# Modulation vectors of a diffusion step: weights as the stationary operand, in spans of 384 columns

## The chip, the cores and the metric

One core of one Trainium2 chip runs the program. The metric is the device time of one execution in microseconds (us). The program was timed three times before the change, and one more execution was taken by the profiler.

## What is computed

The kernel does one step of a two-layer model on 384 tokens of 1024 features: 128 context tokens and 256 latent tokens. Each layer modulates its tokens with nine vectors per conditioning, where there are two conditionings: one for the context tokens, one for the latent ones.

```python
def _layer(x, cond, P, l, h0):
    mod = (jax.nn.silu(cond) @ P['w_mod'][l] + P['b_mod'][l]).reshape(cond.shape[0], N_MOD, 1, D_MODEL)
    sh1, sc1, gt1, sh2, sc2, gt2, sh3, sc3, gt3 = [mod[:, i] for i in range(N_MOD)]
    h = _rmsnorm(x, P['norm_g'][l, 0]) * (1.0 + sc1) + sh1
    x = x + 0.5 * gt1 * _swiglu(h, P['ffn_w1'][l, 0], P['ffn_w2'][l, 0])
    h = _rmsnorm(x, P['norm_g'][l, 1]) * (1.0 + sc2) + sh2
    y, h_final = _mixer(h, P, l, h0)
    x = x + gt2 * y
    h = _rmsnorm(x, P['norm_g'][l, 2]) * (1.0 + sc3) + sh3
    x = x + 0.5 * gt3 * _swiglu(h, P['ffn_w1'][l, 1], P['ffn_w2'][l, 1])
    return x, h_final
```

The matrix `w_mod` has 1024 rows and 9216 columns in each of the two layers, in float32 (75.5 MB in all). A conditioning is one row, so the product is a matrix times two vectors.

## The kernel before

**The main stream.** All tokens are kept feature major (128 features by 384 tokens per tile). The weights of the FFNs and the mixer come from HBM as units of 512 KB through three buffers `wr`, issued by the queue of SP (SyncE). ACT rounds a unit to its upper half `wh` (line 126) and DVE makes the rest `wl` (line 105); both have three buffers. PE then does three matmuls for each block of 128 by 128 weights (lines 198 to 200: upper by upper, upper weights by lower tokens, lower weights by upper tokens), 24 for a unit. The weights are the stationary operand, the 384 tokens move.

**Order.** PE runs in the order in which the code is written. ACT, DVE and SP are also in written order in the opening section; behind it a scheduler orders them. The loads of weights and modulation have high priority once `settled` has run (`ahead()`). Side work is written as generators and added with `track(generator, rate, start)`; `tick()` is called between pieces of the main stream and advances each generator by its rate, from its start tick on.

**The modulation** (`mod_group`, lines 354 to 406). A group is 2048 columns. For each of eight blocks of 128 rows it loads two tiles of 128x1024 into buffers `m6` (four of them; `modw`) and issues four matmuls into four bands of 32 rows of one bank: the stationary operand is `silu_c` (128x32, of which two columns are the conditionings), and the weights move, 512 columns per band (line 386). One such step lies in one tick. At the end ACT copies the bank (line 396), PE transposes it in blocks of 128 columns (line 138), and four DVE adds put bias and result into `mod`. The last group of a layer has 1024 columns and 256 per band. The first 2048 columns of layer 0 are needed at once and are done in two halves of 1024 columns (256 per band), loaded as eight tiles each: rows 0 to 511 in `m6`, the others in `c4` (five buffers). `First.half` then makes the hidden vectors `hh` and `hl` of that half.

**The wide pieces** (`mod_wide`, lines 409 to 438). Columns 2048 to 6143 of layer 1 are made in four pieces of 1024 columns on DVE: for each conditioning a sum `macc` over the eight row blocks, multiplied by the conditioning's number of each partition (ACT for the first block, DVE `scalar_tensor_tensor` for the other seven). Then eight matmuls with the stationary `pick` sum over partitions (line 428), and the result is copied and transposed as above.

**Others that the prediction names.** `token_sums` (line 468) sums squares over partitions: stationary is a block of 32 tokens by 128 partitions, moving is one column of ones, in four bands. Line 1172 is a matmul of the mixer with 128x32 stationary and 48 moving columns. `cacc` is a sum of the mixer's convolution, on DVE.

Of the kernel before, what the change touches and what calls it, by code (L numbers as in the profile page):

```python
# [19 lines left out]
P = 128  # L20
# [36 lines left out]
def hybrid_step(ctx: ExitStack, tc: tile.TileContext, I, pos_r, pos_c, y_prompt, y_sample, new_state):  # L57
# [31 lines left out]
    def c4(shape, name):  # L89
        return sp.tile(shape, F32, tag="c4", name=name, bufs=5)  # L90
# [7 lines left out]
    def m6(shape, name, dt=F32):  # L98
        return mx.tile(shape, dt, tag="m6", name=name, bufs=4)
# [254 lines left out]
    def mod_group(l, q):  # L354

        half = isinstance(q, tuple)
        if half:
            c0 = q[1] * 512
            starts = [c0, c0 + 256, D + c0, D + c0 + 256]
            parts = [I["w_mod"][l][:, :MG].rearrange("r (a b c) -> r a b c", a=2, b=2)[:, :, q[1], :]]  # L360
        else:
            n = min(MG, NMOD * D - q * MG)
            starts = [q * MG + i * n // 4 for i in range(4)]
            parts = [I["w_mod"][l][:, q * MG + c : q * MG + c + WU] for c in range(0, n, WU)]
        w = WU * len(parts) // 4
        nb = w // P

        def load(k):
            raws = []
            for src in parts:  # L370
                raw = c4([P, WU], "modw") if half and k > 3 else m6([P, WU], "modw")
                dst = raw.rearrange("p (a c) -> p a c", a=2) if half else raw
                with ahead():
                    nc.sync.dma_start(dst, src[k * P : (k + 1) * P])
                raws.append(raw)
            return raws

        if half:
            loaded = [load(k) for k in range(KD)]
            yield  # L380
        b = ax_bank()
        for k in range(KD):
            raws = loaded[k] if half else load(k)
            for s in range(4):
                i, c = divmod(s * w, WU)
                pe.matmul(  # L386
                    b[32 * s : 32 * s + 32, :w],
                    silu_c[:, k, :],
                    raws[i][:, c : c + w],
                    start=(k == 0),  # L390
                    stop=(k == KD - 1),
                    skip_group_check=True,
                )
            yield
        ev = sp.tile([P, 512], F32, tag="c2", name="modev", bufs=7)
        act.activation(ev[:, :w], b[:, :w], AF.Copy)
        yield
        b2 = ax_bank()
        for j in range(nb):
            transpose(b2[:, j * P : (j + 1) * P], ev[:, j * P : (j + 1) * P], P)  # L400
        src = b2[:, :w].rearrange("p (b s r) -> p b s r", s=4, r=32)
        for s, c0 in enumerate(starts):
            j0 = c0 // P
            bias = bm_t[l][:, j0 : j0 + nb].unsqueeze(2).to_broadcast([P, nb, 2])
            add(mod_t[l][:, j0 : j0 + nb, :], src[:, :, s, 0:2], bias)

    pick = cst.tile([P, 2, 32], F32, tag="pick", name="pick")
    pool.memset(pick, 0.0)
    for s_ in range(2):
        pool.memset(pick[:, s_, s_ : s_ + 1], 1.0)  # L410

    def mod_wide(l, c0, n=WU):

        acc = [c4([P, WU], f"macc{s}") for s in range(2)]
        for k in range(KD):
            raw = m6([P, WU], "modw")
            nc.sync.dma_start(raw, I["w_mod"][l][k * P : (k + 1) * P, c0 : c0 + WU])
            for s in range(2):
                if k == 0:
                    act.activation(acc[s], raw, AF.Copy, scale=silu_c[:, k, s : s + 1])  # L420
                else:
                    stt(acc[s], raw, silu_c[:, k, s : s + 1], acc[s])
                yield
        w = WU // 4
        b = ax_bank()
        for i in range(2):
            for s in range(4):
                pe.matmul(
                    b[32 * s : 32 * s + 32, :w],
                    pick[:, i, :],  # L430
                    acc[i][:, s * w : (s + 1) * w],
                    start=(i == 0),
                    stop=(i == 1),
                    skip_group_check=True,
                )
        yield
        mod_out(l, b, [c0 + s * w for s in range(4)], w)
        yield

    def mod_out(l, b, starts, w):  # L440
        nb = w // P
        ev = sp.tile([P, 512], F32, tag="c2", name="modev", bufs=7)
        act.activation(ev[:, :w], b[:, :w], AF.Copy)
        b2 = ax_bank()
        for j in range(nb):
            transpose(b2[:, j * P : (j + 1) * P], ev[:, j * P : (j + 1) * P], P)
        src = b2[:, :w].rearrange("p (b s r) -> p b s r", s=4, r=32)
        for s, c0 in enumerate(starts):
            j0 = c0 // P
            bias = bm_t[l][:, j0 : j0 + nb].unsqueeze(2).to_broadcast([P, nb, 2])  # L450
            add(mod_t[l][:, j0 : j0 + nb, :], src[:, :, s, 0:2], bias)
# [1195 lines left out]
    def mod_all(l, qs, after):  # L1647
        for q in qs:
            yield from mod_group(l, q)
            after(l, q)  # L1650

    def mod_wides(l, qs, after):
        for q in qs:
            for c0 in range(q * MG, min((q + 1) * MG, NMOD * D), WU):
                yield from mod_wide(l, c0)
            after(l, q)

    def after_mod(l, q):
        if isinstance(q, tuple):
            norm_scale(l, 0, 4 * q[1], 4 * q[1] + 4)  # L1660
        elif q == 0:
            norm_scale(l, 0)
        elif q == 1:
            gate_scale(l, 0)
        elif q == 2:
            norm_scale(l, 1)
            gate_scale(l, 1)
        elif q == 3:
            norm_scale(l, 2)
        else:  # L1670
            gate_scale(l, 2)

# [50 lines left out]
    mods = mod_all(0, [(0, 0)], after_mod)  # L1723
    with tc.manual_schedule(engines={mybir.EngineType.Activation, mybir.EngineType.DVE, mybir.EngineType.SP}):
# [21 lines left out]
        rest = mod_all(0, [(0, 1)], after_mod)  # L1746
# [28 lines left out]
    for l in range(DEPTH):  # L1775
        if l == 0:
            track(mod_all(0, [1], after_mod), 0.6)
            track(mod_all(0, [2, 3], after_mod), 0.4, 20)
            track(tables(0), 1.9, 8)
        else:  # L1780
            track(tables(1), 1.6, 8)
            track(mod_all(1, [3, 4], after_mod), 0.5, 10)
        nxt = Lead(l, 1)
        ffn(l, 0, 0, ld, nxt, None if l else more)
        ld, nxt = nxt, Lead(l, 2)
        mixer(l, ld, nxt)
        if l == 0:
            track(mod_all(0, [4], after_mod), 1.0)
            track(mod_all(1, [0], after_mod), 0.4, 14)
            track(mod_wides(1, [1, 2], after_mod), 1.2, 4)  # L1790
        ld, nxt = nxt, Lead(l + 1, 0) if l + 1 < DEPTH else Final()
        ffn(l, 1, 2, ld, nxt)
        ld = nxt
# [59 lines left out]
```

## Time and profile before

| | us |
|---|---|
| median of three runs | 1774.3 |
| lowest, highest | 1772.38, 1775.49 |
| profiled execution, its own time | 1775.03 |
| profiled execution, its span | 1773.0 |
| PE busy | 1743.7 (98%) |
| DVE busy | 1246.8 (70%) |
| ACT busy | 795.8 (45%) |
| POOL busy | 203.5 (11%) |

The span reaches from the first to the last recorded instruction; 2.0 us of the execution's own time lie around it. The shares are means over the whole span. A record whose row says "x8" stands for eight records that follow each other with nothing between them. Matmuls overlap: their durations overlap those of their neighbours, so the distance from start to start is what counts.

### The profile page before, as it was taken

What the parts mean: (1) busy time and instruction counts of PE and PEld (TensorE: products, weight loads), DVE (VectorE), ACT (ScalarE), POOL (GpSimd) and SP (SyncE); (2) the same over time, 40 slices, a digit from 0 to 9 for tenths busy, and PEclk for the clock granted to TensorE, in tenths of its full rate; (3) what the DMA queues carried; (4) which work ended last, traced back from release to release, by engine and by line L of the source; (5) the groups of instructions that cost most, each with busy time, mean ns of one, the idle gap of its engine ahead of it and who ended that gap; (6) DMA issues with size and microseconds to landing.
All of it is one profiled execution on the core that took longest, in us unless ns stands there. A gap on an engine that the chain in (4) does not pass through costs nothing.

```text
span 1773.0 us, 30946 instructions
## 1 busy us (share of the span) xinstructions
PE 1743.7 (98%) x12116; PEld 1652.8 (93%) x12116; DVE 1246.8 (70%) x2344; ACT 795.8 (45%) x1330; POOL 203.5 (11%) x400
## 2 busy tenths in 40 slices
PE   7999999999999999999999999999999999999997
PEld 4899999999999989999999899999999999999997
DVE  5496676778986885678487666767799788544435
ACT  3344333575355553233366233336744546423233
POOL 2012343310010000000001133232100000000000
PEclk9999999999999999999999999999999999999999
DMA  9778788776753677788346776667666443444332
GB/s 343 249 224 275 231 252 269 226 198 190 240 157 108 186 238 228 237 280 257 112 131 208 234 224 215 175 195 233 162 210 200 131 123 116 132 130 127 123 125 77
DMA packets 253753, 344.48 MB, mean 194 GB/s; under 512 B 22399, under 2 KB 216651, under 8 KB 253608
## 3 DMA queue, kind: packets, MB, share of 16 engines
q1 hardware_dynamic: 228504, 299.18, 53.4%
q0 software_dynamic: 17088, 39.51, 7.5%
q10 hardware_dynamic: 8016, 3.82, 0.8%
q8 instruction: 95, 1.56, 0.4%
q14 instruction: 50, 0.41, 0.1%
HBM read 309.75 MB, written 32.70 MB: 193 GB/s over the span
## 4 chain that ended last, share of the span: by engine, by line
PE 81%; DVE 10%; ACT 4%; DMA 3%; issue 2%; SPq 0%; ACTq 0%; DVEq 0%
PE mm L198 25%; PE mm L200 25%; PE mm L199 25%; PE ax L386 3%; DVE wl L105 3%; DVE cacc L123 2%; DMA wr<-in_w_gate_dram 1%; DVE m_t L105 1%; PE tb L138 1%; ACT wh L126 1%; DVE m_hh L105 1%; DMA modw<-in_w_mod_dram 1%; DVE macc L123 1%; DMA wr<-in_w_in_dram 1%; ACT zp L1125 0%
## 5 line engine op out<-in xcount | busy, mean ns | idle before, releaser
L105 DVE TENSOR_TENSOR wl<-wr,wh 128x1024 fp32r<-128x1024 f32 (+2 forms) x389 | 457.0, 1175 | 352.1 <-ACT wh L126 347.4
L126 ACT ACTIVATE wh<-wr 128x1024 fp32r<-128x1024 f32 (+1 forms) x387 | 395.9, 1023 | 613.9 <-PE mm L199 443.9
L198 PE MATMUL mm<-hh,wh 128*128 128x384 f32 x1840 | 625.3, 340 | 2.7 <-ACT hh L621 2.7
L200 PE MATMUL mm<-hh,wl 128*128 128x384 f32 x1840 | 617.1, 335 | 4.4 <-DVE wl L105 4.2
L199 PE MATMUL mm<-hl,wh 128*128 128x384 f32 x1840 | 616.3, 335 | 0.5 <-DVE hl L105 0.3
L198 PEld LDWEIGHTS mm<-hh,wh 128*128 128x128 f32 x1840 | 345.9, 188 | 31.7 <-issue 18.1
L200 PEld LDWEIGHTS mm<-hh,wl 128*128 128x128 f32 x1840 | 345.8, 188 | 6.7 <-DVE wl L105 6.7
L199 PEld LDWEIGHTS mm<-hl,wh 128*128 128x128 f32 x1840 | 345.9, 188 | 1.2 <-DVE hl L105 1.1
L198 PE MATMUL mm<-ah,wh 128*128 128x384 f32 x800 | 273.2, 342 | 0.0
L199 PE MATMUL mm<-al,wh 128*128 128x384 f32 x800 | 269.4, 337 | 0.8 <-DVE al L105 0.8
L200 PE MATMUL mm<-ah,wl 128*128 128x384 f32 x800 | 270.0, 338 | 0.0
L198 PEld LDWEIGHTS mm<-ah,wh 128*128 128x128 f32 x800 | 150.2, 188 | 10.2 <-issue 6.7
L199 PEld LDWEIGHTS mm<-al,wh 128*128 128x128 f32 x800 | 150.4, 188 | 1.7 <-DVE al L105 1.1
L200 PEld LDWEIGHTS mm<-ah,wl 128*128 128x128 f32 x800 | 150.2, 188 | 0.0
L123 DVE SCALAR_TENSOR_TENSOR x<-mm,gt,x 128x128 f32<-128x128 f32 x224 | 83.1, 411 | 33.3 <-PE mm L200 33.1
L198 PE MATMUL mm<-xh,wh 128*128 128x386 f32 x240 | 84.7, 353 | 0.0
L126 ACT ACTIVATE ah<-av 128x384 fp32r<-128x384 f32 x82 | 42.1, 519 | 89.4 <-DVE av L105 89.1
L200 PE MATMUL mm<-xh,wl 128*128 128x386 f32 x240 | 81.9, 341 | 0.0
L199 PE MATMUL mm<-xl,wh 128*128 128x386 f32 x240 | 81.9, 341 | 0.0
L123 DVE SCALAR_TENSOR_TENSOR macc<-modw,silu_c,macc 128x1024 f32<-128x1024 f32 x56 | 69.9, 1278 | 14.9 <-DMA modw<-in_w_mod_dram 14.9
L123 DVE SCALAR_TENSOR_TENSOR cacc<-pad,pv,cacc 128x399 f32<-128x399 f32 x120 | 69.7, 627 | 0.0
L386 PE MATMUL ax<-modw,silu_c 128*32 128x512 f32 (+1 forms) x576 | 63.2, 511 | 0.7 <-DMA modw<-in_w_mod_dram 0.7
(316 smaller groups left out, 1820.0 us busy)
## 6 DMA issues: line engine op xcount, KB each, us to landing
wr<-in_ffn_w_dram SPq DMA_DIRECT2D x256, 512.0 KB, 3.6
modw<-in_w_mod_dram SPq DMA_DIRECT2D x144, 512.0 KB, 5.4
wr<-in_w_gate_dram SPq DMA_DIRECT2D x48, 512.0 KB, 3.8
wr<-in_w_in_dram SPq DMA_DIRECT2D x24, 512.0 KB, 3.6
my<-my POOLq DMA_DIRECT2D x16, 512.0 KB, 5.5
ms<-ms POOLq DMA_DIRECT2D x16, 512.0 KB, 4.9
m_ms<-ms SPq DMA_DIRECT2D x16, 512.0 KB
m_my<-my SPq DMA_DIRECT2D x16, 512.0 KB, 7.4
```

The lines of the kernel that those rows point to most:

```text
L105: (eng or dve).tensor_tensor(out, a, b, op=op)
L123: dve.scalar_tensor_tensor(out, a, s, b, op0=op0, op1=op1)
L126: act.activation(hi, full, AF.Copy)
L138: pe.transpose(out, in_, ident[:rows, :rows])
L198: pe.matmul(out, wh[:, k, cols], xh, start=first, stop=False)
L199: pe.matmul(out, wh[:, k, cols], xl, start=False, stop=False)
L200: pe.matmul(out, wl[:, k, cols], xh, start=False, stop=last)
L386: pe.matmul(b[32 * s : 32 * s + 32, :w], silu_c[:, k, :], raws[i][:, c : c + w], start=(k == 0), stop=(k == KD - 1), skip_group_check=True,)
```

## The change

The two start halves stay as they were (`mod_half`). All other groups of columns become `mod_cols`: spans of 384 columns. A span is loaded by two DMAs of 128x4x384 (768 KB, rows of 1536 bytes) into two `m6` buffers, one span ahead of its use. In one tick PE then issues 96 matmuls for it: a block of 128x32 weights is stationary, the two columns of `silu_c` move, four bands of 32 rows, eight row blocks summed. The result is feature major, as `mod` is, and one DVE add gives it the bias (`mod_done`). There is no copy, no transpose.

The wide pieces (`mod_wides`) are now five of 768 columns (2048 to 5887 of layer 1), with loads of 128x768 into buffers `c3` (`modv`), and the sum over partitions takes the blocks of `macc` as stationary, one column of ones moving: 48 matmuls. The rest of layer 1 (5888 to 9215) is done by `mod_cols` in the first FFN of layer 1. The rates and start ticks of the tracks change, too.

```diff
...
+    def mod_done(l, c0, n, b):
+
+        add_bias(l, c0, n, b[:, : 2 * (n // P)].rearrange("p (j s) -> p j s", s=2))
+        for i in range(NMOD):
+            if c0 < (i + 1) * D <= c0 + n:
+                if i % 3 == 1:
+                    norm_scale(l, i // 3)
+                elif i % 3 == 2:
+                    gate_scale(l, i // 3)
+
+    def mod_cols(l, c0, c1):
+
+        spans = [(c, min(NT, c1 - c)) for c in range(c0, c1, NT)]
+
+        def load(c, n):
+            raws = []
+            for h in range(2):
+                raw = m6([P, 4, n], "modw")
+                src = I["w_mod"][l][4 * h * P : 4 * (h + 1) * P, c : c + n]
+                with ahead():
+                    nc.sync.dma_start(raw, src.rearrange("(k p) c -> p k c", p=P))
+                raws.append(raw)
+            return raws
+
+        nxt = load(*spans[0])
+        yield
+        for i, (c, n) in enumerate(spans):
+            raws = nxt
+            if i + 1 < len(spans):
+                nxt = load(*spans[i + 1])
+            yield
+            b = ax_bank()
+            for j in range(n // P):
+                for k in range(KD):
+                    for r in range(0, P, 32):
+                        pe.matmul(
+                            b[r : r + 32, 2 * j : 2 * j + 2],
+                            raws[k // 4][:, k % 4, j * P + r : j * P + r + 32],
+                            silu_c[:, k, 0:2],
+                            start=(k == 0),
+                            stop=(k == KD - 1),
+                            skip_group_check=True,
+                        )
+            mod_done(l, c, n, b)
+            yield
+
+    WW = 768
+
+    def mod_wides(l, c0, c1):
+
+        for c in range(c0, c1, WW):
+            acc = [c4([P, WW], f"macc{s}") for s in range(2)]
+            for k in range(KD):
+                raw = c3([P, WW], "modv")
+                nc.sync.dma_start(raw, I["w_mod"][l][k * P : (k + 1) * P, c : c + WW])
+                for s in range(2):
+                    if k == 0:
+                        act.activation(acc[s], raw, AF.Copy, scale=silu_c[:, k, s : s + 1])
+                    else:
+                        stt(acc[s], raw, silu_c[:, k, s : s + 1], acc[s])
+                    yield
+            yield
+            b = ax_bank()
             for s in range(2):
...
+                for j in range(WW // P):
+                    for r in range(0, P, 32):
+                        pe.matmul(
+                            b[r : r + 32, 2 * j + s : 2 * j + s + 1],
+                            acc[s][:, j * P + r : j * P + r + 32],
+                            ones[:, 0:1],
+                            start=True,
+                            stop=True,
+                            skip_group_check=True,
+                        )
+            mod_done(l, c, WW, b)
+            yield
 
     def mod_vec(l, i):
         return mod_t[l][:, 8 * i : 8 * i + 8, :]
...
     track(other_vectors(), 0.25, 8)
     for l in range(DEPTH):
         if l == 0:
-            track(mod_all(0, [1], after_mod), 0.6)
-            track(mod_all(0, [2, 3], after_mod), 0.4, 20)
+            track(mod_cols(0, 2 * D, 8 * D), 0.55, 2)
             track(tables(0), 1.9, 8)
         else:
             track(tables(1), 1.6, 8)
-            track(mod_all(1, [3, 4], after_mod), 0.5, 10)
+            track(mod_cols(1, 5888, NMOD * D), 0.36, 8)
         nxt = Lead(l, 1)
         ffn(l, 0, 0, ld, nxt, None if l else more)
         ld, nxt = nxt, Lead(l, 2)
         mixer(l, ld, nxt)
         if l == 0:
-            track(mod_all(0, [4], after_mod), 1.0)
-            track(mod_all(1, [0], after_mod), 0.4, 14)
-            track(mod_wides(1, [1, 2], after_mod), 1.2, 4)
+            track(mod_cols(0, 8 * D, NMOD * D), 1.0)
+            track(mod_cols(1, 0, 2 * D), 0.4, 14)
+            track(mod_wides(1, 2 * D, 5888), 1.6, 4)
         ld, nxt = nxt, Lead(l + 1, 0) if l + 1 < DEPTH else Final()
         ffn(l, 1, 2, ld, nxt)
         ld = nxt
...
```

**SP, the opening.** These are the DMA issues of SP in order from the first half's loads on (`128x2x512` are the loads of the halves, `wr` weight units, `128x1024` and `128x4x384` the loads of later columns). Before:

```order
4 L149 DMA wr<-in_ffn_w_dram 128x4x256 x2
5 L374 DMA modw<-in_w_mod_dram 128x2x512 x8
6 L149 DMA wr<-in_ffn_w_dram 128x4x256 x2
7 L374 DMA modw<-in_w_mod_dram 128x1024 x6
8 L149 DMA wr<-in_ffn_w_dram 128x4x256 x4
```

With the change:

```order
4 L149 DMA wr<-in_ffn_w_dram 128x4x256 x2
5 L364 DMA modw<-in_w_mod_dram 128x2x512 x6
6 L418 DMA modw<-in_w_mod_dram 128x4x384 x4
7 L364 DMA modw<-in_w_mod_dram 128x2x512 x2
8 L149 DMA wr<-in_ffn_w_dram 128x4x256 x11
9 L418 DMA modw<-in_w_mod_dram 128x4x384 x2
```

Four loads of the first two spans stand between the sixth and the seventh load of the second half, and the weight units follow behind the half.

**PE, the first FFN of layer 0.** One step of the old form between matmuls of the main stream (`mm`), before:

```order
112 L198 MATMUL mm<-hh_536,wh 128x384
113 L199 MATMUL mm<-hl_537,wh 128x384
114 L200 MATMUL mm<-hh_536,wl 128x384
115 L386 MATMUL ax<-modw,silu_c 32x512 x4
116 L198 MATMUL mm<-hh_354,wh 128x384
117 L199 MATMUL mm<-hl_355,wh 128x384
118 L200 MATMUL mm<-hh_354,wl 128x384
```

The first burst of the new form, with the change:

```order
206 L200 MATMUL mm<-hh_532,wl 128x384
207 L198 MATMUL mm<-hh_532,wh 128x384
208 L199 MATMUL mm<-hl_533,wh 128x384
209 L200 MATMUL mm<-hh_532,wl 128x384
210 L433 MATMUL ax<-silu_c,modw 32x2 x96
211 L198 MATMUL mm<-hh_350,wh 128x384
212 L199 MATMUL mm<-hl_351,wh 128x384
213 L200 MATMUL mm<-hh_350,wl 128x384
```

The bursts stand further apart than the steps did, and each has 24 times as many matmuls.

**DVE, the mixer of layer 0.** `wl` is the conversion of a weight unit that PE waits for, the others are the mixer's own work. Before, behind the end of the convolution's sums:

```order
736 L105 TENSOR_TENSOR wl<-wr,wh 128x1024
737 L105 TENSOR_TENSOR al<-zp,ah 128x384
738 L105 TENSOR_TENSOR wl<-wr,wh 128x1024
739 L123 SCALAR_TENSOR_TENSOR y_6086<-zp,pv_311,tb 128x384
740 L105 TENSOR_TENSOR wl<-wr,wh 128x1024
741 L123 SCALAR_TENSOR_TENSOR ga<-ga,y_6086 128x384
742 L105 TENSOR_TENSOR zp<-y_6086,ga 128x384
743 L105 TENSOR_TENSOR al<-zp,ah 128x384
744 L105 TENSOR_TENSOR wl<-wr,wh 128x1024 x3
```

With the change, at the same place:

```order
748 L105 TENSOR_TENSOR wl<-wr,wh 128x1024
749 L105 TENSOR_TENSOR al<-zp,ah 128x384
750 L123 SCALAR_TENSOR_TENSOR macc_8997<-modv,silu_c,macc_8997 128x768
751 L123 SCALAR_TENSOR_TENSOR macc_8998<-modv,silu_c,macc_8998 128x768
752 L123 SCALAR_TENSOR_TENSOR macc_8997<-modv,silu_c,macc_8997 128x768
753 L105 TENSOR_TENSOR wl<-wr,wh 128x1024
754 L123 SCALAR_TENSOR_TENSOR macc_8998<-modv,silu_c,macc_8998 128x768
755 L123 SCALAR_TENSOR_TENSOR macc_8997<-modv,silu_c,macc_8997 128x768
756 L123 SCALAR_TENSOR_TENSOR macc_8998<-modv,silu_c,macc_8998 128x768
757 L123 SCALAR_TENSOR_TENSOR y_7486<-zp,pv_307,tb 128x384
758 L105 TENSOR_TENSOR wl<-wr,wh 128x1024
```

The first wide sums (`macc`) stand here between the conversions; 31 of all 70 do so before the mixer ends. Before, the first of them was row 909, after the mixer.

## Rows read from the trace of the kernel before

**Rows 1.** The page: busy time by engine, and the chain that ended last.
```profile
PE 1743.7 (98%) x12116; PEld 1652.8 (93%) x12116; DVE 1246.8 (70%) x2344; ACT 795.8 (45%) x1330; POOL 203.5 (11%) x400
...
PE 81%; DVE 10%; ACT 4%; DMA 3%; issue 2%; SPq 0%; ACTq 0%; DVEq 0%
```

**Rows 2.** PE timeline, 140 to 142 us: start, duration, line, operation, tiles, count.
```profile
140.29 0.34 PE L200 MATMUL mm<-ah,wl 128*128 128x384 f32 x1
140.56 1.06 PE L386 MATMUL ax<-modw,silu_c 128*32 128x512 f32 x8
...
142.01 0.34 PE L200 MATMUL mm<-ah,wl 128*128 128x384 f32 x1
142.18 0.34 PE L198 MATMUL mm<-ah,wh 128*128 128x384 f32 x1
```

**Rows 3.** PE timeline, 28 to 30 us.
```profile
28.40 0.34 PE L200 MATMUL mm<-hh,wl 128*128 128x384 f32 x1
28.67 0.64 PE L386 MATMUL ax<-modw,silu_c 128*32 128x256 f32 x8
...
29.70 0.35 PE L200 MATMUL mm<-hh,wl 128*128 128x384 f32 x1
```

**Rows 4.** PE timeline, 114 to 116 us.
```profile
114.72 0.34 PE L200 MATMUL mm<-ah,wl 128*128 128x384 f32 x1
114.90 0.60 PE L138 MATMUL ax<-ident,modev 128*128 128x128 f32 x4
...
115.69 0.34 PE L200 MATMUL mm<-ah,wl 128*128 128x384 f32 x1
```

**Rows 5.** PE timeline, 36 to 43 us.
```profile
36.84 1.07 PE L386 MATMUL ax<-modw,silu_c 128*32 128x256 f32 x16
...
42.43 0.44 PE L198 MATMUL mm<-hh,wh 128*128 128x384 f32 x1 [0.71 <-ACT hh L621]
```

**Rows 6.** PE timeline, 543 to 545 us.
```profile
543.34 0.34 PE L200 MATMUL mm<-hh,wl 128*128 128x384 f32 x1
543.61 0.37 PE L468 MATMUL ax<-ones,csq 128*32 128x1 f32 x24
...
544.36 0.34 PE L200 MATMUL mm<-hh,wl 128*128 128x384 f32 x1
```

**Rows 7.** Lines 468 and 1172 by themselves: shortest, median and longest record, ns.
```profile
L468 PE MATMUL ax<-ones,csq x48: 170/170/191, 543.6 to 1411.6; 128*32 128x1 f32 x48
...
L1172 PE MATMUL tb<-U,m_ms x1024: 206/206/230, 403.7 to 1331.8; 128*32 128x48 f32 x171
```

**Rows 8.** PE timeline, 403 to 405 us.
```profile
403.69 0.89 PE L1172 MATMUL tb<-U,m_ms 128*32 128x48 f32 x64
```

**Rows 9.** Tiles macc and cacc: shortest, median, longest ns; first and last start.
```profile
L123 DVE SCALAR_TENSOR_TENSOR macc<-modw,silu_c,macc x56: 1271/1277/1287, 648.5 to 833.2; 128x1024 f32<-128x1024 f32 x56
...
L123 DVE SCALAR_TENSOR_TENSOR cacc<-pad,pv,cacc x120: 604/628/640, 427.3 to 1383.0; 128x399 f32<-128x399 f32 x120
```

**Rows 10.** Timeline of SP's DMA queue, 25 to 42 us (duration: of the issues).
```profile
25.14 3.12 SPq L149 DMA_DIRECT2D wr<-in_ffn_w_dram  x2
29.37 12.71 SPq L374 DMA_DIRECT2D modw<-in_w_mod_dram  x6
```

**Rows 11.** Windows: length, busy PE, PEld, DVE, ACT, POOL, clock, DMA share, GB/s.
```profile
24.00:29.00 5.00, 4.85 (x26) 4.14 (x25) 4.48 (x10) 2.33 (x4) 0.00 (x0) 0.71 1.05 387
```

**Rows 12.** Windows, 358 to 365 us.
```profile
358.00:361.30 3.30, 1.34 (x30) 1.00 (x29) 2.44 (x6) 3.08 (x8) 0.57 (x1) 1.00 1.08 377
361.30:365.00 3.70, 3.70 (x14) 3.70 (x13) 3.67 (x11) 0.46 (x2) 0.00 (x0) 0.54 0.84 281
```

**Rows 13.** Window, 517 to 582.5 us.
```profile
517.00:582.50 65.50, 65.50 (x394) 64.39 (x393) 44.65 (x76) 34.31 (x53) 0.54 (x1) 1.00 0.45 140
```

**Rows 14.** Timelines of DVE and PE, 581 to 583 us.
```profile
581.30 1.22 DVE L105 TENSOR_TENSOR wl<-wr,wh 128x1024 fp32r<-128x1024 f32 x1
...
582.69 0.34 PE L200 MATMUL mm<-hh,wl 128*128 128x384 f32 x1
```

More of the change, by code (lines that the diff above doesn't have):

```diff
@@ L352, in hybrid_step, with mod_half @@
     gt_t = [[cst.tile([P, KD, 2], F32, tag=f"gt{l}{i}", name=f"gt{l}{i}") for i in range(3)] for l in range(DEPTH)]
[L354 to L366, printed above, removed]
-        def load(k):
[L369 to L380, printed above, removed]
+    def mod_half(l, half):
+        c0 = half * 512
+        starts = [c0, c0 + 256, D + c0, D + c0 + 256]
+        part = I["w_mod"][l][:, : 2 * D].rearrange("r (a b c) -> r a b c", a=2, b=2)[:, :, half, :]
+        w = 256
+        def load(k):
+            raw = c4([P, WU], "modw") if k > 3 else m6([P, WU], "modw")
+            with ahead():
+                nc.sync.dma_start(raw.rearrange("p (a c) -> p a c", a=2), part[k * P : (k + 1) * P])
+            return raw
+        loaded = [load(k) for k in range(KD)]
+        yield
         b = ax_bank()
         for k in range(KD):
-            raws = loaded[k] if half else load(k)
             for s in range(4):
-                i, c = divmod(s * w, WU)
                 pe.matmul(
@@ L388, in mod_group @@
                     silu_c[:, k, :],
-                    raws[i][:, c : c + w],
+                    loaded[k][:, s * w : s * w + w],
                     start=(k == 0),
@@ L394, in mod_group @@
             yield
+        nb = w // P
         ev = sp.tile([P, 512], F32, tag="c2", name="modev", bufs=7)
@@ L402, in mod_group @@
         for s, c0 in enumerate(starts):
[L403 to L417, printed above, removed]
-            for s in range(2):
[L419 to L451, printed above, removed]
+            add_bias(l, c0, w, src[:, :, s, 0:2])
@@ new lines, in mod_half, with add_bias @@
+        norm_scale(l, 0, 4 * half, 4 * half + 4)
+    def add_bias(l, c0, n, src):
+        j0, nb = c0 // P, n // P
+        bias = bm_t[l][:, j0 : j0 + nb].unsqueeze(2).to_broadcast([P, nb, 2])
+        add(mod_t[l][:, j0 : j0 + nb, :], src, bias)
+    def mod_done(l, c0, n, b):
[6 more added lines that the diff above has]
+                    gate_scale(l, i // 3)
@@ new lines, in mod_cols @@
+    def mod_cols(l, c0, c1):
[5 more added lines that the diff above has]
+                src = I["w_mod"][l][4 * h * P : 4 * (h + 1) * P, c : c + n]
+                with ahead():
+                    nc.sync.dma_start(raw, src.rearrange("(k p) c -> p k c", p=P))
[22 more added lines that the diff above has]
+            yield
@@ new lines, in hybrid_step @@
+    WW = 768
[13 more added lines that the diff above has]
+            b = ax_bank()
+            for s in range(2):
+                for j in range(WW // P):
[9 more added lines that the diff above has]
+            mod_done(l, c, WW, b)
+            yield
@@ L1644, in mixer @@
                 nxt.raw()
[L1647 to L1671, printed above, removed]
     def tables(l):
@@ L1722, in hybrid_step @@
     ld = First()
-    mods = mod_all(0, [(0, 0)], after_mod)
+    mods = mod_half(0, 0)
     with tc.manual_schedule(engines={mybir.EngineType.Activation, mybir.EngineType.DVE, mybir.EngineType.SP}):
@@ L1745, in hybrid_step @@
         prefetch(1)
-        rest = mod_all(0, [(0, 1)], after_mod)
+        rest = mod_half(0, 1)
         next(rest)
```

## Prediction

> **What bounds the kernel now.** I read the page first: PE is busy 98% of the span and holds 81% of the chain that ended last [rows 1]. So an insertion into PE's stream costs what it delays the next matmul, and a wait costs only if PE runs dry. Next I read the PE timeline around each kind of insertion. In the plain stream a matmul of 384 columns starts every 0.17 us (142.01, then 142.18 in [rows 2]). The price of an insertion is the time from the last start before it to the third start after it, less three such spacings (0.52): the third, because the first two starts after an insertion are still late. Last I looked at the two places where the new order of instructions differs on a queue that PE waits for: SP's queue in the first 45 us, and DVE's in the mixer of layer 0.
>
> **PE, removed.** A step of the old form (four bands, 512 columns moving) costs 142.01 − 140.29 − 0.52 = 1.20 us [rows 2]; one of 256 columns 29.70 − 28.40 − 0.52 = 0.78 us [rows 3]; four transposes of the evacuated result 115.69 − 114.72 − 0.52 = 0.45 us [rows 4], 0.11 each. By the code five groups of 2048 columns go with eight steps of 512 each, and two groups of 1024 with eight steps of 256; the two start halves stay. So 40 × 1.20 + 16 × 0.78 = 60.5 go. The 32 transposes outside the halves (five groups of four, two of two, and two for each of four wide pieces) are 3.5. The four picks of the wide pieces each have eight matmuls of 256 columns, per band as many columns as one step of 512, so 4 × 1.20 = 4.8. That is 68.8. One step of 512 is free today (it lies in the time in which PE waits for the token vectors until 42.43, [rows 5]), and some eight insertions stand directly beside another one and pay the entry and exit, 0.31 (below), only once: 2.5. Removed: **65.0 us**.
>
> **PE, added.** The new form has stationary weights of 128x32 and one or two moving columns. The same form exists: the token sums (L468) are 24 records of 128x32 with one column. They cost 544.36 − 543.34 − 0.52 = 0.50 us [rows 6]; the row is 0.37 long and one record 0.17, so 24 records start within 0.20, 8.3 ns each [rows 6, 7], and entry and exit are the other 0.30. One fp32 matmul is two records (a step is four matmuls in the code and eight records in [rows 2]). A span of 384 columns is 3 × 8 × 4 = 96 matmuls, 192 records: 1.60 and 0.31 make 1.91 us. There are 31 such bursts, two of 64 matmuls (1.37 each), one of 32 (0.84) and five wide ones of 48 (1.11 each): 59.2 + 2.7 + 0.8 + 5.6 = 68.3, less some six shared entries, 1.8: **66.5 us**. Net **+1.5**. The bounds: the insertion with 64 records of the same weights and 48 columns is 0.89 long [rows 8] with records of 0.21 [rows 7], so 10.7 ns each; by that the 6,752 new records (31 × 192 + 2 × 128 + 64 + 5 × 96 are 6,752) cost 2.4 ns × 6,752 = 16 more, net +18. Below, 7.3 ns, since the 0.37 is a rounded row and its first pass is longer than the others: net −5. I take 8.3, the row that is nearest in columns.
>
> [...]
>
> **DVE and ACT.** The wide pieces were 56 DVE multiply-adds of 1024 columns at 1.277 us [rows 9]; now 70 of 768. Between this row and the 0.628 at 399 columns [rows 9] it comes to 1.01 us each (estimate): 71 us, before 71.5. The evacuations and three of four adds go; they ran beside PE's 98% and are worth nothing by themselves.
>
> **Start (SP's queue).** Before, SP issues all eight loads of the second half, then the next weight units, and then six modulation loads from 29.37 on as buffers come free [rows 10]. Now four loads of 786 KB stand ahead of the last two loads of that half (0.52 MB each), and the next weight units behind these. The four wait for buffers that PE frees with the half's first steps, so the last two can't be issued early. From 29.37 there are 4 × 0.786 + 2 × 0.524 = 4.19 MB ahead of the end of the half, 10.9 us at the 387 GB/s that the queue moves here [rows 11]: 40.3, and about 42 with what is still in flight. PE does these two steps at 36.84 and waits for their result until 42.43 already [rows 5]. So PE stops for about 5, and one conversion of a late weight unit (1 to 2 us) joins the chain that follows: **+7** (5 to 11). [...]
>
> **Mixer of layer 0 (DVE's queue).** Before, the first wide multiply-add runs at 648.5, after the mixer [rows 9]. Now 31 of the 70 stand on DVE among the conversions (wl) that lie between 517 and 567 before. They need 31 × 1.01 = 31.3 us. From 517 to 582.5 DVE is busy 44.65 of 65.5, so it has 20.85 idle [rows 13]. At 582.5 there is no slack left: the wl that ends at 582.52 is used by PE at 582.69 [rows 14]. So PE loses 31.3 − 20.85 = **+10.5**. It could be 6, if DVE's idle time after a wait on PE shrinks when PE is late, or 16, if the weights of the wide pieces arrive late and hold DVE's queue. In the FFN behind it DVE has less to do than before; PE is the bound there, so I count nothing back.
>
> **Sum.** 1775.0 + 1.5 + 7 + 1.5 + 10.5 = 1795.5 for the profiled execution's own time; the median of the runs shown is 0.7 lower than that execution, so **1795**. Its own range is 1783 to 1812.
>
> **Rivals.**
> *A, the bursts starve or cool PE.* Each burst is almost two microseconds in which the array gets hardly a column, 34 times (and five shorter). If such a stretch acts on the clock as the idle 2 us from 358 did [rows 12], each could cost up to 1.7 us: +58. Or a long run of tiny records is fed more slowly than 24 of them: each further ns per record is 6.75 us. For it: no run of 192 such records exists in the trace. Against it: 64 of them pass at 10.7 ns [rows 8] and the plain stream is 0.17 us per matmul right behind. With half of the bursts hit, +29 on top: about 1825. [...]
> *B, the stalls are covered.* SP's four loads come early enough and DVE's additional work fits its idle time, since the waits at 582 come from PE's own products. Then only the net of PE is left: 1775.8, within 0.2% (3.5 us, about what a measurement of this kernel can tell from no change), 1771 to 1778.
> *C, faster.* One mechanism: four bands of tiny matmuls overlap more fully than in [rows 6], so that the bursts run at 7 ns a record or less. At 7.3 ns the net is −5, at 6 ns −14. With covered stalls the first gives 1769 and the second 1761. The point from which it decides is 7.6 ns a record with covered stalls, and 4.7 ns with the stalls as above. For it: [rows 6] is the only price, and its 0.20 holds an entry of its own. Against it: the longer row of the same weights has more, not less [rows 8]. That the change doesn't do what it says I exclude: in the new order the bursts stand where the steps stood, and only the halves keep the old form.
>
> **How the numbers follow.** The forecast 0.53, A 0.15, B 0.13, C 0.19. The forecast and A are slower by over 0.2%: 0.68. B is no change: 0.13. C is faster: 0.19. The range leaves out the upper half of A and the lower half of C: 1765 to 1822.
>
> **What would show it.** PE's rows: 34 bursts with 1.9 us from the last start before to the third after, 0.31 of it not in the records. A PE stop from about 37 to 42 with the half's last modulation load as releaser, and the second one at the hl and hh behind it. DVE busy at 95% or more from 517 to 590 and PE waiting for wl there, some 10 us in all. The forecast is wrong if PE's granted clock falls behind bursts (A), if the two stops are under 3 us each (B), or if a burst costs less than 1.5 us (C).

## The result, and the profile after

The changed kernel takes **1865.67 us** (median of four runs, 1863.82 to 1867.66), against 1774.57 for the kernel before in the same comparison: a ratio of 1.0515 (95% interval 1.0497 to 1.0534), 91 us slower. The prediction was 1795 with a range from 1765 to 1822. The direction was right; most of the loss was not in the sum.

The page of the kernel after, first the lines that answer to [rows 1], then the clock by slices and the instruction queue:

```profile
span 1863.8 us, 43321 instructions
...
PE 1783.2 (96%) x18324; PEld 1731.1 (93%) x18324; DVE 1248.4 (67%) x2353; ACT 790.6 (42%) x1321; POOL 202.6 (11%) x397
...
PEclk8889899999999999999999999999999999999999
...
q8 instruction: 143, 2.34, 0.5%
...
PE 79%; DVE 10%; issue 4%; DMA 3%; ACT 3%; POOL 0%; SPq 0%; DVEq 0%; ACTq 0%
```

PE is still the bound, with 40 us more of busy time in 91 us more of span. The share of "issue" in the chain has doubled, from 2% [rows 1] to 4%: an engine waits, and the profile shows nothing that it waits for. In the waits of PE, this is now the first line (in the kernel before, "issue" had 0.7 us, once):

```profile
PE ax L433 <- issue: 25.3, 12, 4.0
PE ax L372 <- DMA modw<-in_w_mod_dram: 6.8, 3, 6.2
PE mm L198 <- ACT hh L643: 6.5, 2, 4.5
PE mm L200 <- DVE wl L105: 5.7, 10, 1.4
...
PE mm L199 <- issue: 5.4, 2, 3.1
PE mm L198 <- issue: 4.7, 3, 2.4
...
PE ax L464 <- issue: 1.9, 1, 1.9
...
PE tb L138 <- issue: 1.3, 1, 1.3
```

The columns are the time in all, the number of waits and the longest one. Line 433 is the burst. Two "issue" rows on the main stream's lines, 5.4 and 4.7 us, come on top, and one stop each in two other groups of small matmuls (lines 464 and 138): 38.6 us in 19 stops.

To see where the time went I cut both executions at the same five matmuls of the main stream (counted on the matmuls that use `wl`) and read the windows between them: opening, first FFN, mixer, second FFN, first FFN of layer 1, the rest. Columns: window, length, busy PE, PEld, DVE, ACT, POOL, granted clock, DMA share, GB/s. The kernel before:

```profile
0.00:62.50 62.50, 50.25 (x355) 36.42 (x356) 32.17 (x74) 27.20 (x50) 10.83 (x30) 0.97 0.93 323
62.50:385.60 323.10, 321.14 (x2132) 295.65 (x2131) 234.42 (x545) 143.03 (x250) 87.55 (x168) 0.99 0.76 241
385.60:641.90 256.30, 254.05 (x2145) 243.26 (x2144) 215.64 (x414) 139.81 (x250) 15.33 (x28) 1.00 0.58 177
641.90:911.50 269.60, 268.78 (x1608) 255.21 (x1608) 186.31 (x277) 96.84 (x133) 0.54 (x1) 1.00 0.68 220
911.50:1248.50 337.00, 337.00 (x2249) 318.40 (x2248) 237.91 (x446) 157.67 (x279) 79.33 (x154) 1.00 0.67 205
1248.50:1773.00 524.50, 512.48 (x3638) 503.86 (x3636) 340.39 (x593) 231.20 (x374) 9.88 (x19) 0.99 0.46 139
```

And after:

```profile
0.00:74.50 74.50, 52.15 (x331) 40.63 (x332) 32.24 (x74) 25.82 (x48) 10.41 (x27) 0.82 0.75 254
74.50:436.40 361.90, 342.30 (x5023) 332.62 (x5023) 236.23 (x549) 142.22 (x248) 87.42 (x168) 0.94 0.71 219
436.40:701.40 265.00, 256.49 (x2489) 245.50 (x2488) 243.84 (x450) 142.45 (x254) 15.89 (x29) 1.00 0.66 204
701.40:983.50 282.10, 274.17 (x3073) 270.86 (x3072) 162.16 (x257) 101.15 (x145) 5.87 (x18) 0.98 0.58 191
983.50:1340.80 357.30, 345.32 (x3781) 337.47 (x3780) 234.02 (x435) 148.15 (x258) 73.18 (x136) 0.98 0.60 186
1340.80:1863.80 523.00, 512.77 (x3637) 503.98 (x3635) 339.95 (x593) 230.81 (x373) 9.85 (x19) 0.99 0.45 139
```

The lengths grow by 12.0, 38.8, 8.7, 12.5 and 20.3 us; the rest is 1.5 shorter. The three FFN windows, where all but two of the bursts are, lose 71.6. In the first of them PE is idle for 19.6 us (before 2.0), and the clock is 0.94, which costs another 18 us against 0.99 (estimate): together 36 of the 38.8. In the mixer the clock is full, DVE has 28.2 us more work and PE 8.5 us of idle time (before 2.3).

A burst that doesn't stop costs what the prediction said. On the PE timeline of the kernel after, the first burst:

```profile
82.31 0.34 PE L200 MATMUL mm<-hh,wl 128*128 128x384 f32 x1
82.58 1.78 PE L433 MATMUL ax<-silu_c,modw 128*32 128x2 f32 x192
...
84.74 0.34 PE L200 MATMUL mm<-hh,wl 128*128 128x384 f32 x1
```

From 82.31 to the third start behind, 84.74, less 0.52, is 1.91 us: the predicted number. The second burst is different:

```profile
101.69 1.75 PE L433 MATMUL ax<-silu_c,modw 128*32 128x2 f32 x188
105.57 0.28 PE L433 MATMUL ax<-silu_c,modw 128*32 128x2 f32 x4 [2.13 <-issue]
...
106.58 0.52 PE L200 MATMUL mm<-hh,wl 128*128 128x384 f32 x1
106.90 0.52 PE L198 MATMUL mm<-hh,wh 128*128 128x384 f32 x1
```

188 of its 192 records run at the same pace, then PE stands for 2.1 us, and the stream behind runs at 0.32 us per matmul instead of 0.17. That is the clock at half, and the window behind the stop shows it, at 0.50:

```profile
106.60:110.00 3.40, 3.40 (x12) 3.40 (x11) 3.40 (x30) 0.00 (x0) 0.00 (x0) 0.50 0.97 322
```

The opening answers to [rows 5] and [rows 10]. PE and SP of the kernel after:

```profile
44.55 1.08 PE L372 MATMUL ax<-modw,silu_c 128*32 128x256 f32 x8 [6.19 <-DMA modw<-in_w_mod_dram]
...
54.16 0.69 PE L198 MATMUL mm<-hh,wh 128*128 128x384 f32 x1 [4.47 <-ACT hh L643]
...
30.85 4.43 SPq L418 DMA_DIRECT2D modw<-in_w_mod_dram  x4
...
35.32 1.45 SPq L364 DMA_DIRECT2D modw<-in_w_mod_dram  x2
```

The second-last step of the second half waits 6.2 us for the half's last loads, which SP issues behind the four loads of the spans (line 418). The first matmul of the main stream that needs this half comes at 54.16 instead of 42.43.

### The profile page after: what moved, and what is told of

Read it like the earlier page. It is cut to its first block, busy times and chain, and to the rows that moved or that the text cites. A ratio compares the mean times of both kernels' runs of the same rounds, so it can differ in the third digit from the quotient of the medians.

```text
span 1863.8 us, 43321 instructions
## 1 busy us (share of the span) xinstructions
PE 1783.2 (96%) x18324; PEld 1731.1 (93%) x18324; DVE 1248.4 (67%) x2353; ACT 790.6 (42%) x1321; POOL 202.6 (11%) x397
## 3 DMA queue, kind: packets, MB, share of 16 engines
q8 instruction: 143, 2.34, 0.5%
## 4 chain that ended last, share of the span: by engine, by line
PE 79%; DVE 10%; issue 4%; DMA 3%; ACT 3%; POOL 0%; SPq 0%; DVEq 0%; ACTq 0%
PE mm L198 24%; PE mm L199 24%; PE mm L200 24%; PE ax L433 3%; DVE wl L105 2%; DVE cacc L123 2%; PE tb L138 1%; DVE m_t L105 1%; ACT wh L126 1%; DVE m_hh L105 1%; DVE macc L123 1%; DMA wr<-in_w_gate_dram 1%; DMA wr<-in_ffn_w_dram 1%; DMA wr<-in_w_in_dram 0%; DVE acc L105 0%
## 5 line engine op out<-in xcount | busy, mean ns | idle before, releaser
L198 PE MATMUL mm<-hh,wh 128*128 128x384 f32 x1840 | 634.8, 345 | 9.5 <-ACT hh L643 6.5
L200 PE MATMUL mm<-hh,wl 128*128 128x384 f32 x1840 | 627.3, 341 | 5.5 <-DVE wl L105 5.4
L199 PE MATMUL mm<-hl,wh 128*128 128x384 f32 x1840 | 626.7, 341 | 5.6 <-issue 5.4
L198 PEld LDWEIGHTS mm<-hh,wh 128*128 128x128 f32 x1840 | 354.1, 192 | 14.2 <-ACT hh L643 7.1
L200 PEld LDWEIGHTS mm<-hh,wl 128*128 128x128 f32 x1840 | 353.8, 192 | 12.0 <-DVE wl L105 8.7
L199 PEld LDWEIGHTS mm<-hl,wh 128*128 128x128 f32 x1840 | 354.5, 193 | 5.4 <-issue 4.2
L433 PEld LDWEIGHTS ax<-silu_c,modw 128*32 128x32 f32 x6272 | 57.5, 110 | 34.6 <-issue 32.8
L433 PE MATMUL ax<-silu_c,modw 128*32 128x2 f32 x6272 | 61.5, 173 | 25.3 <-issue 25.3
L123 DVE SCALAR_TENSOR_TENSOR macc<-modv,silu_c,macc 128x768 f32<-128x768 f32 x70 | 69.7, 1013 | 3.2 <-DMA modv<-in_w_mod_dram 2.8
```

The lines of the kernel that those rows point to most:

```text
L123: dve.scalar_tensor_tensor(out, a, s, b, op0=op0, op1=op1)
L198: pe.matmul(out, wh[:, k, cols], xh, start=first, stop=False)
L199: pe.matmul(out, wh[:, k, cols], xl, start=False, stop=False)
L200: pe.matmul(out, wl[:, k, cols], xh, start=False, stop=last)
L433: pe.matmul(b[r : r + 32, 2 * j : 2 * j + 2], raws[k // 4][:, k % 4, j * P + r : j * P + r + 32], silu_c[:, k, 0:2], start=(k == 0), stop= ...
```

## What the stops are

**Theory: instructions.** The page counts 143 packets with 2.34 MB on the instruction queue, 16 KB each. PE ran 18,324 matmul records and as many weight loads, 36,648 instructions: 256 for each packet. The page of the kernel before has 95 for its 24,232 instructions, 255 each:

```profile
q8 instruction: 95, 1.56, 0.4%
```

So here PE's instructions arrive in blocks of 256. In the plain stream, with two instructions per 0.173 us, a block lasts 22 us. In a burst it lasts 128 records × 8.3 ns = 1.1 us. Counted on the trace, twice the number of the matmul record at which PE stops is 176, 174, 168, 160, 152 and 148 modulo 256 for six bursts of the first FFN that stop: one place in a block, drifting slowly with the instructions that the trace leaves out. All 19 stops lie on this drift, which goes from 176 down to 56, those in the two other groups of small matmuls included. A burst has 384 instructions, so about half of all bursts hold two borders. By this place 14 of the 31 do; 12 of these stop at the second border, and the other two have the first border within about their first 11 instructions. The five stops of the main stream lie up to 13 records behind a burst, at the border that follows the one inside it.

With 1.1 us between the borders and 2.2 us of stop a fetch takes some 3.3 us (estimate), if it begins at the border before. The packets of the instruction queue, which the trace has with their times, show the fetches. At every one of the 19 stops one packet lands 1.2 to 2.1 us before PE goes on. It took 0.9 to 1.5 us, and it had started between 0.9 us before and 2.5 us after PE passed the border before. At the second burst PE passes this border at 102.20, the packet runs from 103.27 to 104.22, and PE goes on at 105.57. No packet starts less than 2.4 us after the end of the one before. That a fetch begins at the border before is the author's estimate; the packets show its start only to within these 3.4 us.

**Rivals.** *Clock:* the clock falls because a burst has hardly any columns, stop or no stop. *Weights:* the second tile of a span is late. For the start and the mixer the theories are the prediction's.

## The experiments

**1. All borders moved by 128 instructions.**

```diff
+        pad = ax_bank()
+        for i in range(32):
+            r = 32 * (i % 4)
+            pe.matmul(
+                pad[r : r + 32, 0:2], ones[:, 0:32], ones[:, 0:2], start=True, stop=True, skip_group_check=True,
+            )
```

> The changed kernel with 32 tiny matmuls (64 records and 64 weight loads, 128 instructions of PE) put into PE's idle time in the opening; everything behind them stays. They leave nothing out. Instruction theory: PE's instructions arrive in blocks of 256, the next block is asked for only when the one before it is begun, and a fetch takes some 3.3 us; a burst of 384 instructions that holds two borders of blocks stops at the second one. Moving all borders by 128 instructions then swaps the bursts: of the first fourteen the 1st, 5th, 6th, 10th, 11th and 13th, which ran through in 1.6 us, now stop for 0.7 to 4 us, and the 2nd, 3rd, 4th, 8th, 12th and 14th, which stopped, run through. The time stays within 15 us of 1866, as about half of the bursts stop in either. Clock theory (the array cools because a burst has hardly any columns) and weights theory (the second tile of weights is late): the same bursts stop as before, time 1866 plus or minus 4.

Measured: 1871.7 us, a single run. The first and the second burst on the PE timeline:

```profile
80.65 1.51 PE L433 MATMUL ax<-silu_c,modw 128*32 128x2 f32 x161
84.37 0.60 PE L433 MATMUL ax<-silu_c,modw 128*32 128x2 f32 x31 [2.21 <-issue]
...
103.64 1.78 PE L433 MATMUL ax<-silu_c,modw 128*32 128x2 f32 x192
105.35 0.44 PE L198 MATMUL mm<-hh,wh 128*128 128x384 f32 x1
```

They have swapped: the first stops for 2.2 us, the second runs through. Of the first fourteen, the 1st, 6th, 10th, 11th and 13th now stop, and the 2nd, 3rd, 8th, 12th and 14th run through; the 4th has lost its stop of 1 us but for 0.4. One is missed: the 5th runs through, and PE stops for 3.1 us from about 1 us behind it on. Its second border lies 5 records behind its end. Behind the 4th, too, PE stops for 2.0 us, at a border 14 records behind its end. The "issue" stops of this run, too, lie on one drifting place, from 180 to 60 modulo 256. Weights and columns are the same in both runs, so neither makes the stop.

**2. Bursts of 192 instructions.** The rates of the other three `mod_cols` tracks rise by the same factor of 1.5.

```diff
+                    if (j * KD + k + 1) % 12 == 0 and j * KD + k + 1 < n // P * KD:
+                        yield
...
-            track(mod_cols(0, 2 * D, 8 * D), 0.55, 2)
+            track(mod_cols(0, 2 * D, 8 * D), 0.825, 2)
```

> The changed kernel with each span of 384 columns issued in two bursts of 48 matmuls (192 instructions) in two ticks instead of one of 96, with the rates of these tracks raised so that they end at the same place. Instruction theory: 192 instructions can't hold two borders of 256, so the stops in and behind the bursts go (about 37 us by the starts around each burst) and with them the stretches at the lower clock behind (about 26 us); 31 further entries and exits cost 0.3 us each, 9 us. Time 1805 to 1820. Clock theory: twice as many stretches with few columns, the low clock stays: 1850 to 1875. Weights theory: the second half of the rows is used later than before, so some stops shrink, but whichever stops are for the first tile stay: 1840 to 1875.

Measured: 1805.53 us (1803.84 to 1805.71), ratio to before 1.017 (1.0155 to 1.0185), 60 us less than the change. "issue" at the burst's line falls from 25.3 us to 1.7:

```profile
PE ax L433 <- issue: 1.7, 1, 1.7
```

and the window from the first burst nearly to the end of the first FFN has the full clock:

```profile
72.00:400.00 328.00, 325.97 (x5003) 314.83 (x5002) 231.46 (x540) 136.74 (x236) 87.32 (x168) 0.99 0.77 241
```

The three FFN windows lose 12.2 us against before instead of 71.6. A burst of 48 costs 1.11 us wherever the main stream stands on both sides of it. So few columns for 0.8 us, some sixty times, did not lower the clock here; the low stretches came with the stops. In the trace of the kernel after, behind the opening and up to the last 10 us, 15 stretches have the lower level: each begins during one of the 19 stops or within 2 us behind it.

**3. The first two spans' loads behind the half's.**

```diff
-                with ahead():
+                with (ahead() if c > 2 * D + NT else nullcontext()):
```

> The changed kernel, but the loads of the first two spans have no high priority, so that SP issues all eight loads of the second start half, and three weight units, ahead of them. Order of PE unchanged. Start theory: PE's stop before the last two steps of the half (6.2 us) and the longer wait behind it go, the second half's first matmul starts at about 42.5 again instead of 54.2, and the time falls by 11 to 13 us, to 1853 to 1855. Rival: the first bursts then wait for their weights, or the clock behind the stop was most of it, and less than 5 us come back.

Measured: 1849.92 us (1848.21 to 1854.72), ratio 1.0429 (1.041 to 1.0449), 15.7 less. PE waits for no load of the half now:

```profile
39.06 1.07 PE L372 MATMUL ax<-modw,silu_c 128*32 128x256 f32 x16
...
44.52 0.61 PE L198 MATMUL mm<-hh,wh 128*128 128x384 f32 x1 [2.93 <-ACT hh L643]
```

The opening is 0.9 us longer than before instead of 12.0, so 11.1 as expected; the other 4 to 5 us came in later windows, where the bursts still stop, for a little less time (first FFN +35.5 instead of +38.8).

**4. The wide pieces' weights in `m6`.**

```diff
-                raw = c3([P, WW], "modv")
+                raw = m6([P, WW], "modv")
```

> The changed kernel with the weights of the wide pieces in the buffers m6 instead of c3, so that none of the 70 wide sums stands on DVE in the mixer of layer 0 any more (the first comes in the second FFN, as in the kernel before). Order of PE unchanged. DVE theory: the 8 us by which PE fell back in that mixer come back, time 1856 to 1860. Rival: PE's delay there comes from fetches of instructions or other waits and nothing comes back (1864 to 1868), or the wide sums then compete with the spans for m6 in the second FFN and it is slower.

Measured: 1872.02 us (1865.45 to 1880.91): nothing gained, and it doesn't decide. The mixer gave back 7 us, and the second FFN took 11 more: the sums are now late, and PE waits for them in its fixed order:

```profile
PE ax L433 <- issue: 26.2, 13, 4.4
PE ax L464 <- DVE macc L123: 13.4, 2, 8.0
```

**5. Experiments 2 and 3 together.** Both edits.

> The two edits together: bursts of 48 matmuls, and the first two spans' loads without high priority. The two losses lie in different places, so both gains should add: 1805.5 less 13 to 16 is 1789 to 1793. Rival: part of what the later loads gave came from the clock behind the bursts' stops, which are gone here, and less than 8 us come: 1797 or more.

Measured: 1794.9 us (1794.3 to 1797.42), ratio 1.0118 (1.0103 to 1.0133): 10.6 less than experiment 2, between theory and rival. The opening gives 10.0 of it. The rest of experiment 3's gain lay in windows with stops, and it doesn't come where the bursts don't stop.

**6. Three bursts of 32.** As 5, with `% 8` for `% 12` and higher rates.

> As e5, but three bursts of 32 matmuls (128 instructions) in three ticks for each span. It measures entry and exit: instruction theory says that nothing is left to gain from shorter bursts, and 31 further entries cost 0.3 us each, so 9 us more than e5: about 1800. Rival: what is left over the kernel before still comes from instructions arriving late or from the clock, and shorter bursts take some of it away: no slower than e5, 1780 to 1791.

Measured: 1804.21 us (1803.13 to 1808.61), 9.3 more than 5: by the medians 0.3 us for each of 31 further entries (by the two traces the FFN windows grow by 6.4). Shorter bursts have nothing left to give. One stop of 2.5 us is left, directly behind a burst.

**7. Weights over the whole array.** As 3, without bands:

```diff
-                    for r in range(0, P, 32):
...
+                        b[:, 2 * j : 2 * j + 2],
+                        raws[k // 4][:, k % 4, j * P : (j + 1) * P],
```

> As e3 (one burst for each span, first loads later), but with 128x128 weights stationary over the whole array instead of four bands of 32: 24 matmuls, 48 records and 96 instructions for a span. Instruction theory: no burst can hold two borders of 256 instructions, so no stops in or behind bursts, which by e2 is worth some 63 us against e3's 1850. [...] Clock theory: the low clock stays behind bursts, as they last longer with as few columns.

Measured: 1995.79 us, a single run. No stop in any burst, as expected. No row of an earlier run has the price of a record of this form; by the starts it takes 0.11 us at the full clock and 0.21 at half. The first burst on the PE timeline, 8.24 us long against 1.78 with four bands:

```profile
71.71 8.24 PE L432 MATMUL ax<-silu_c,modw 128*128 128x2 f32 x48
```

The windows ahead of this burst, in it and behind it:

```profile
68.00:71.70 3.70, 3.70 (x23) 3.70 (x22) 1.54 (x2) 0.63 (x1) 0.00 (x0) 1.00 0.43 131
71.70:79.60 7.90, 7.90 (x49) 7.90 (x48) 0.76 (x2) 1.88 (x3) 0.00 (x0) 0.64 0.21 55
79.60:82.00 2.40, 2.40 (x9) 2.40 (x10) 2.01 (x4) 0.00 (x0) 0.00 (x0) 0.50 0.90 285
```

Here the clock falls inside the burst, with no stop: 0.64 over 7.9 us, 0.50 behind it. So what the clock theory says did happen in these bursts; those of four bands, 0.8 or 1.6 us long, that ran through have no slow stretch behind them in the traces of the kernel after and of experiment 2, unless PE stops there.

**8. The kernel before, with three pieces more on DVE.** The price of a wide piece (a pick and two transposes, 1.42 us of PE for 1024 columns, beside 5.0 to 6.5 in steps with their transposes) and DVE's idle time in the first FFN of layer 1 suggested it.

```diff
-            track(mod_all(1, [3, 4], after_mod), 0.5, 10)
+            track(mod_wides(1, [3, 4], after_mod), 1.0, 10)
```

> The kernel before, with the last three pieces of 1024 columns of layer 1 made on DVE as the four wide pieces are, in the first FFN of layer 1, instead of 8 steps of 512 and 8 of 256 columns on PE. PE loses 8 x 1.20 + 8 x 0.78 + 0.45 + 0.22 = 16.5 us of insertions and gets three picks with two transposes, 3 x 1.42 = 4.3 us; DVE gets 42 sums of 1.28 us, 54 us, beside 90 us in which it is idle between 960 and 1180. If DVE's idle time takes them, the time falls by 12 us to about 1763. Rival: the sums stand ahead of conversions that PE waits for, as in the mixer of layer 0, and it is no faster (1772 or more).

Measured: 1767.96 us (1765.4 to 1768.63), ratio 0.9959 (0.9945 to 0.9973): faster than the kernel before and the changed one, by 7 of the expected 12. At 1157 on the clock of the kernel before PE was 10 us ahead of it. By 1234 it had lost 5 of them: the last piece's pick stands there, and PE waits 1.9 us for the token sums' input (line 468).

**9. As 5, the first wide piece alone in `m6`.**

```diff
-                raw = c3([P, WW], "modv")
+                raw = (m6 if c == c0 else c3)([P, WW], "modv")
```

> As e5, with the weights of the first wide piece alone in the buffers m6 and those of the other four in c3, so that no wide sum stands on DVE in the mixer of layer 0 (the first comes with the second FFN) and the pieces compete with the spans for m6 only once. DVE theory: e5 falls back by 7 to 9 us in that mixer, and this comes back: 1785 to 1789. Rival: the sums are now late in the second FFN, PE waits for macc at the sum over partitions as it did in e4 (13 us there), and it is no faster than e5's 1795.

Measured: 1791.28 us (1787.09 to 1793.73), 3.6 less than 5 by the medians, whose ranges come close. The mixer's window by itself is clear. Experiment 5, then this one:

```profile
394.30:659.20 264.90, 256.80 (x2488) 245.58 (x2487) 244.12 (x450) 143.86 (x255) 15.89 (x29) 1.00 0.67 205
```

```profile
394.50:652.50 258.00, 254.99 (x2489) 245.85 (x2488) 217.05 (x418) 140.81 (x251) 15.89 (x29) 1.00 0.61 187
```

27 us of DVE's work left the window and it is 6.9 us shorter: 1.7 over before's 256.3 instead of 8.6. The sums do cost the mixer these 7 us; the other windows differ by 1 us or less.

**10 and 11. More of the same on the kernel before.** Experiment 10 has rate 1.4 from tick 2 for the three pieces; experiment 11 then also makes columns 0 to 2047 of layer 1 on DVE, in the second FFN (`mod_wides(1, [0, 1, 2], after_mod), 1.9, 2`).

> As e8, with the three pieces at rate 1.4 from tick 2 on instead of 1.0 from tick 10, so that their sums end before the mixer of layer 1. In e8 PE was 10 us ahead of the kernel before at 1150 and lost 4 to 5 of them where the last sums ran: they stay, 1763 to 1765. Rival: the sums then meet the mixer's tables on DVE and PE waits for conversions earlier, 1768 or more.

> As e10, with the first 2048 columns of layer 1 on DVE, too, in the second FFN of layer 0 (six pieces there instead of four, rate 1.9): PE loses 8 x 1.20 + 0.45 = 10 us and gets 2 x 1.42 = 2.8, so 7 less, 1756 to 1758, if the 36 us of further sums fit into the 82 us in which DVE is idle there from 640 to 907. Rival: the last sums end late for the start of layer 1, which needs just these columns, and PE waits for them: 1764 or more.

Measured: 1767.66 us (1767.21 to 1768.68), the same as experiment 8: the loss ahead of the mixer went, but so did some of the gain. With six pieces there 1763.77 us (1762.1 to 1765.96), ratio 0.9937 (0.9923 to 0.9952): **the fastest version, 11 us under the kernel before by the ratio.** Its page against [rows 1]: PE 18 us less, DVE 80 more.

```profile
PE 1725.8 (98%) x12004; PEld 1651.0 (94%) x12004; DVE 1327.2 (75%) x2422; ACT 807.6 (46%) x1342; POOL 202.3 (11%) x400
```

## Why the prediction was wrong

- *PE, removed and added (net +1.5): right, as far as it went.* A burst that runs through costs 1.91 us, as said, and one of 48 costs 1.11. The 192 records of the first burst, in four bands, start within 1.61 us, 8.4 ns each, where 8.3 was taken. In experiment 2, where all but one burst run through, the three FFN windows lose 12.2 us: 1.5 of net work, 10 for 33 further entries (the two spans of 256 columns are split, too), and 0.8 more of idle time. Two sums of the prediction are off by 0.1 (65.1 for 65.0 removed, 10.8 us for 10.9 of loads), which changes nothing.
- *The step that failed* is the sentence "A span of 384 columns is … 192 records: 1.60 and 0.31 make 1.91 us", multiplied by 31. It took a burst of 384 instructions for eight insertions of 24 records in a row. Half of the bursts stop for their own instructions, in or directly behind the burst, and the clock falls at the stops. In the three FFN windows PE's idle time grows by 36.7 us, and the lower clock costs some 30 more (estimate, half of PE's busy time at that level): 67 of the 71.6 lost there. Experiment 2 takes both away and pays 10 for its further entries, so that 59 us come back. The row was there: the page before has 95 packets for 24,232 instructions.
- *Rival A* named it ("a long run of tiny records is fed more slowly"), with a chance of 0.15. Its price, 1825, took half of the bursts at 1.7 us; a stop costs about 2 us (38.6 in 19), and the clock at it some 1.6 more. In the plain stream, where a block lasts 22 us, crossing a border is all but free (one "issue" wait of 0.7 us in the whole kernel before); where a block lasts 1.1 us, the crossing costs the 19 stops.
- *Start: right, and larger.* +8.5 with the clock was forecast, +12.0 came, within the 5 to 11 for the stop and 1.5 for the clock; experiment 3 takes 11.1 back. No run shows the second 1.5 of the sum, the one for the clock: from 54.2 to 60.7 the granted clock is 0.50, which takes about 3.3 us (estimate, half of the 6.5).
- *Mixer: right in place and size.* +10.5 (6 to 16) forecast, +8.7 measured, and 6.9 of it by experiment 9. DVE is busy 72.4 of 73 us from 568 to 641, the stretch that is 517 to 590 in the kernel before. A sum of 768 columns takes 1.012 us (1.01 said). The waits are other than forecast: PE waits 3.9 us for `wl` in this window (1.4 before), not 10, and 3.6 for three results of ACT (`cs`, `gt`, `ah`), which are there in time again in experiment 9. Two bursts fall into this window, too: PE's busy time in it is 2.4 us longer.
- *Rivals B and C.* B needed covered stalls, and C those or records of 4.7 ns; both stalls came, and a record takes 8.4.

Open: why the stops differ so much (0.6 to 4.0 us). The start of the packet varies by 3.4 us against the border before; what delays it isn't shown. In the one stop of experiment 2 it starts 4.8 us behind that border. Open, too, is whether a burst of 96 placed by its position in the block would save the 10 us of further entries. That wasn't tried.

## What to carry to other kernels

Price a long run of tiny instructions twice: by its rows, and by how many instructions an engine gets through before the next block of them can be there. The page's instruction queue against the count of instructions gives the block (here 36,648 instructions in 143 packets, 256 each), and the time that a block lasts in the plain stream, against the time in a burst, shows how much slack is left for its fetch (here 22 us against 1.1). Bursts of less than one block were enough here: of 19 stops with 384 instructions one was left with 192 (experiment 2). And where an engine is the bound, as PE is here at 98%, a sum that costs it the same in another form gains nothing (net +1.5 us for PE here): moving the sum to an engine with idle time, at a place where its queue is not on the path, did (experiment 11, ratio 0.9937).

## What the runs showed of the hardware that was not expected

- By the pages of the two kernels one packet carries 256 (after) and 255 (before) of PE's instructions, and no two overlap: in the trace of the kernel after a packet starts at the earliest 2.4 us after the end of the one before. The 19 stops of 0.6 to 4.0 us are at the second border in or directly behind a run of small matmuls, and PE goes on 1.2 to 2.1 us after the packet's landing. In bursts of 192 instructions one stop of 1.7 us is left.
- The clock fell in a stretch in which PE never stops: 0.64 in 7.9 us of records with two columns (experiment 7).
- A load of 128x128 weights in float32 with two moving columns takes 0.11 us per record at the full clock (experiment 7); four bands of 32 take 33 ns for the four records that cover the same block (8.4 ns each in the kernel after). So bands are faster here by a factor of three, with only two columns moving.
